# Routing the last two tiles from rows without norm, by folded router weights

## The chip, the cores and the metric

The kernel runs on one core of one Trainium2 chip. The metric is the device time of one execution in microseconds. Three runs of the kernel before gave 1399.96 us as median (1399.85 to 1399.97).

The engines are TensorE (PE; its weight loads are PEld), VectorE (DVE), ScalarE (ACT), GpSimd (POOL) and SyncE (SP), which here only issues transfers. Each has a queue of its own that it works off in order, and waits on semaphores for the others.

## The reference, cut to what matters

One decoder layer over 1024 tokens of 1024 columns. The change touches the end of the first half and the router of the mixture of experts:

```python
x = layer_norm(DN_ALPHA * x + merged @ w_out[l], ln1_g[l], ln1_b[l])
# hierarchical_moe(x): the best of 4 groups, then the best 2 of its 8 experts
glog = (xt @ w_rg + b_rg)                  # 4 columns
gval, gsel = lax.top_k(glog, 1)
elog = (xt @ w_re + b_re)                  # 32 columns
top_v, top_i = lax.top_k(elog_of_the_group, 2)
weights = softmax(glog)[gsel] * softmax(top_v)
y[token] = sum over its 2 experts of weight * (silu(x @ w_gate) * (x @ w_up)) @ w_down
x = layer_norm(DN_ALPHA * x + y, ln2_g[l], ln2_b[l])
```

The norm is `(u - mean) * rstd * g + b`. The 36 router logits of a token can therefore also be had from its row `u` without norm: with `W' = g * W`, from which the mean of its columns over the 1024 rows is taken, they are `rstd * (u @ W') + (b @ W + bias)`.

## The kernel before, in words

The stages are: projections and attention, the linear recurrence, mixing (up to some 740 us of the profiled execution), the experts (from 767), and the second norm at the end. All products in 32 bits are made of three TensorE passes over a high and a low part (lines 103 to 105); ScalarE makes the high part (L98), VectorE the low one (L99).

**Mixing** (`mixing`) works on 1024 tokens in two halves. A half has 8 branch products and then, for each of its 4 tiles of 128 tokens, two products with `w_out`, one for each 512 columns (`project`). Every product is cut in two parts of 12 passes or more, and such a part is a *tick*; ticks 0 to 63 hold all 32 products. Everything else is put in by tick: `before` holds loads, `stages` what follows a first part, `late_stages` what follows the tick's `post`. The engines' queues are in exactly this written order (`all_order`). After a tile's second product VectorE adds alpha times x and takes statistics (L840, L841, L918), GpSimd makes 1/sqrt (L701), and one or more ticks later `norm` scales the row (four operations, L925 and L926), and `store` writes it to HBM twice, as `x1d`, from which the experts' rows are gathered, and as `zd`, to which their results are added.

**Routing** (`router`) works on batches of two tiles, in five steps whose ticks stand in `BATCHES`: `turn` transposes the normed row (TensorE) and copies it out of PSUM (ScalarE); `logits` multiplies it by the 36 router columns; `choose` turns the logits back and finds group and experts by some 27 small VectorE operations; `place` ranks each token among those of its expert; `enter` adds a matmul to the table of places, which lies in PSUM. From the table `slots` takes the 32 lists of token numbers (`gi`, L1060) and starts the first two gathers of rows (L1086). All of `pa`, one bank of PSUM, is shared by logits, choices and ranks.

**Weights of the experts** are read in 384 pieces of 0.5 MB by SP's queue (`fetch`), into 36 buffers that they share with the tiles of mixing. Ten pieces are fetched in ticks 48 to 60, eight behind tile 6's store and ten behind tile 7's, 28 in all, before the experts begin. SP's queue also holds the stores of the normed rows. Behind the router stands a branch for experts of more than 128 tokens (`overflow`, L1377), which isn't taken; every engine reads one value for it, and at its end SP waits for all transfers that it has issued. Then a piece is fetched for each that is used. At the end of the queue, behind the last piece, stand the loads of `z` for the second norm (`final`).

`warm(n)` issues n small matmuls without use, after the ticks in `WARM`.

The code lines of the profile (L...) are those of this listing.

Of the kernel before, what the change touches and what calls it, by code (L numbers as in the profile page):

```python
# [5 lines left out]
F32 = mybir.dt.float32  # L6
F32R = mybir.dt.float32r
I32 = mybir.dt.int32
AF = mybir.ActivationFunctionType
ALU = mybir.AluOpType  # L10
AX = mybir.AxisListType
# [4 lines left out]
D = 1024  # L16
NE = 32
ALPHA = 2.0 ** 0.25
LN_EPS = 1e-5
# [42 lines left out]
class Builder:  # L62
# [48 lines left out]
    def warm(self, n):  # L111

        if n:
            ps = self.bank("mm")
            for _ in range(n):
                self.nc.tensor.matmul(ps[:, 0:128], self.c("ident"), self.c("ident"), start=True, stop=True)

    WARM = {63: 11, 65: 5, 66: 14, 67: 5}

    def pe_order(self):  # L120
        return self.tc.manual_schedule(engines={mybir.EngineType.PE})
# [641 lines left out]
    def mixing(self):  # L763


        nc = self.nc
        g1, b1 = self.x4(name="ln1_g"), self.x4(name="ln1_b")
        self.wr = self.tile([128, 8, 36], F32, "wr", 1)
        self.br = self.tile([36, 1], F32, "br", 1)

        def constants():
            for t, name in ((g1, "ln1_g"), (b1, "ln1_b")):
                nc.sync.dma_start(t, self.a[name].partition_broadcast(128))
            nc.sync.dma_start(self.wr, self.a["w_r"].rearrange("(k p) c -> p k c", p=128))
            nc.sync.dma_start(self.br, self.a["b_r"][:, None])

        self.asum = None
        self.table = self.bank("tb", (128, 64))
# [9 lines left out]
        def at(d, b, fn):  # L788
            d.setdefault(b, []).append(fn)
# [35 lines left out]
        def project(b, i, c):  # L825
            ps = self.bank("mm")
            s = slice((i % 4) * 128, (i % 4) * 128 + 128)
            for k in range(8):
                h, l = mg[k // 2]
                wh, wl = wo[4 * c + k // 2]  # L830
                self.mm3(ps, h[:, k % 2, s], l[:, k % 2, s], wh[:, k % 2], wl[:, k % 2], k == 0, k == 7)
                if k == 3:
                    yield
            if c == 0:
                u[i] = self.x4(name="u"), self.tile([128, 2, 6], F32, "lst", 2)

            def post():
                t, st = u[i]
                cs = slice(c * 512, c * 512 + 512)
                nc.vector.scalar_tensor_tensor(t[:, cs], xr[i][:, cs], ALPHA, ps, op0=ALU.mult, op1=ALU.add)  # L840
                nc.vector.bn_stats(st[:, c], t[:, cs])  # L841
                if c == 1:
                    mv = self.stats(st, LN_EPS)
                    self.at(2 * b + 2, lambda: norm(2 * b + 2, i, t, mv), True)

            return post

        def norm(b, i, t, mv):
            for c in range(2):
                self.scale(t, mv, g1, b1, c)  # L850
            self.at(b + 2 * (i < 7), lambda: store(i, t))
            batch = next(g for g in self.BATCHES if i in g[0])
            if i == batch[0][0]:
                self.batch = self.router(batch[0])
            for n, d in enumerate(batch[1]):
                fn = self.batch[n]
                if n < 2:
                    self.at(b + d, lambda fn=fn: fn(i, t))
                elif i == batch[0][-1]:
                    self.late_stages.setdefault(b + d, []).append(fn)  # L860

        def store(i, t):
            for d in (self.x1d, self.zd):
                nc.sync.dma_start(d[i * 128:i * 128 + 128, :], t)

        main = []
# [20 lines left out]
                at(before, b, lambda b: self.fetch())  # L887

        at(before, 6, lambda b: constants())
        tick, gen = 0, None  # L890
        while tick < 2 * len(main) or stages or self.late_stages:
            post = None
            if tick < 2 * len(main):
                if tick % 2 == 0:
                    for fn in before.pop(tick // 2, []):
                        fn(tick // 2)
                    gen = main[tick // 2](tick // 2)
                    next(gen)
                else:
                    post = self.run(gen)  # L900
            due = stages.get(tick, [])
            while due:
                due.pop(0)()
            stages.pop(tick, None)
            if post:
                post()
            for fn in self.late_stages.pop(tick, []):
                fn()
            self.warm(self.WARM.get(tick, 0))
            tick += 1  # L910
            if tick >= 2 * len(main) - 1:
                for _ in range(4 if tick < 2 * len(main) + 1 else 2):
                    self.fetch(True)

    def stats(self, st, eps):

# [17 lines left out]
    def small(self, n, nm, bufs=1):  # L934
        return self.tile([128] + (list(n) if isinstance(n, tuple) else [n]), F32, "r" + nm, bufs)

    BATCHES = ((0, 1), (4, 5, 6, 10, 14)), ((2, 3), (4, 5, 6, 10, 14)), ((4, 5), (2, 3, 4, 6, 7)), ((6, 7), (1, 2, 2, 3, 4))

    def router(self, batch):


        nc, vec, t = self.nc, self.nc.vector, self.small
        V = {}
# [1 line left out]
        n = len(batch)  # L945
        lT = self.tile([36, n, 128], F32, "rlT", 1)

        def turn(i, x1):
            V["xT", i] = []
            for j in range(2):  # L950
                ps = self.bank("pb", (128, 4, 128))
                for k in range(4):
                    nc.tensor.transpose(ps[:, k], x1[:, (4 * j + k) * 128:(4 * j + k + 1) * 128], self.c("ident"))
                xT = self.tile([128, 4, 128], F32, "rxT", 2)
                nc.scalar.copy(xT, ps)
                V["xT", i].append(xT)

        def logits(i, _):
            lg = self.pa[0:36, 0:128]
            for j, xT in enumerate(V.pop(("xT", i))):  # L960
                for k in range(4):
                    nc.tensor.matmul(lg, self.wr[:, 4 * j + k], xT[:, k], start=j + k == 0, stop=j == 1 and k == 3)
            nc.scalar.activation(lT[:, i - batch[0]], lg, AF.Identity, bias=self.br)

        def first_max(vals, w, nm, ix):

            mx = t((n, 1), nm + "m")
            vec.tensor_reduce(mx, vals, axis=AX.X, op=ALU.max)
            c = t((n, w), nm + "c")
            for k in range(n):  # L970
                vec.scalar_tensor_tensor(c[:, k], vals[:, k], mx[:, k], low[:, 0:w], op0=ALU.is_ge, op1=ALU.mult)
            vec.tensor_reduce(ix, c, axis=AX.X, op=ALU.min)
            return mx

        def choose():
            l = self.pa[:, 128:128 + 36 * n].rearrange("p (n c) -> p n c", n=n)
            for k in range(n):
                nc.tensor.transpose(l[:, k], lT[:, k], self.c("ident")[0:36, 0:36])
            gl, el = l[:, :, 0:4], l[:, :, 4:36]
            gi = t((n, 1), "gi")  # L980
            gm = first_max(gl, 4, "g", gi)
            em, ge, gs, d = t((n, 32), "em"), t((n, 4), "ge"), t((n, 1), "gs"), t((n, 1), "dd")
            for k in range(n):
                vec.tensor_scalar(em[:, k], self.c("group"), gi[:, k], -3.0e38, op0=ALU.not_equal, op1=ALU.mult)
            vec.tensor_sub(ge, gl, gm.to_broadcast([128, n, 4]))
            nc.scalar.activation(ge, ge, AF.Exp)
            vec.tensor_add(em, em, el)
            eid = self.eid[:, batch[0]:batch[0] + n]
            oh = t((n, 2, 32), "oh")
            ms = []  # L990
            for j in range(2):
                ms.append(first_max(em, 32, "ab"[j], eid[:, :, j:j + 1]))
                for k in range(n):
                    vec.tensor_scalar(oh[:, k, j], low, eid[:, k, j:j + 1], None, op0=ALU.is_equal)
                for k in range(n if j == 0 else 0):
                    vec.scalar_tensor_tensor(em[:, k], oh[:, k, 0], -3.0e38, em[:, k], op0=ALU.mult, op1=ALU.add)
            asg = t((n, 32), "asg")
            vec.tensor_add(asg, oh[:, :, 0], oh[:, :, 1])
            vec.tensor_sub(d, ms[1], ms[0])
            nc.scalar.activation(d, d, AF.Exp)  # L1000
            sums = [self.asum]
            for k in range(n):
                new = t(32, "sum", 6)
                if sums[-1] is None:
                    vec.tensor_copy(new, asg[:, k])
                else:
                    vec.tensor_add(new, sums[-1], asg[:, k])
                sums.append(new)
            self.asum = sums[-1]
            vec.tensor_reduce(gs, ge, axis=AX.X, op=ALU.add)  # L1010
            V["r"] = asg, oh, sums, gs, d

        def place():
            asg, oh, sums, gs, d = V["r"]
# [468 lines left out]
def arrays(inputs):  # L1483
# [10 lines left out]
        "w_out": f["w_out"][0],  # L1494
        "ln1_g": f["ln1_g"][0],
        "ln1_b": f["ln1_b"][0],
        "w_r": np.concatenate([f["router_group_w"][0], f["router_expert_w"][0]], axis=1),
        "b_r": np.concatenate([f["router_group_b"][0], f["router_expert_b"][0]]),
        "w_g": gate_up(f["w_exp_gate"][0]),
# [20 lines left out]
```

## Time and profile before

| | |
|---|---|
| median of three runs | 1399.96 us |
| profiled execution | 1399.95 us |
| its span | 1398.2 us |
| TensorE busy | 1335.6 us (96%) |
| VectorE busy | 1080.5 us (77%) |
| ScalarE busy | 789.4 us (56%) |
| bytes of all transfers | 327.84 MB, 234 GB/s on the mean |

All times are from the span's start; 1.75 us of the profiled execution lie around the span. An engine that is busy nearly all the time isn't thereby the bound: matmuls are pipelined and their ends modelled, and stages differ. In the rows further down, a window's DMA share is the mean busy share of the core's 16 DMA engines; a timeline row has start, length, engine, line, operation, out<-in with shapes, how many are merged (x2), and in brackets the idle time of the engine before it with what ended it; a row of waits has who waited <- for whom: total us, times, longest.

### The profile page before, as it was taken

To read this page: it belongs to the slowest core of one execution; us is meant where nothing else is said; L and a number is where in the kernel's file an instruction comes from. 1 tells how busy PE (TensorE), PEld (TensorE's weight loads), DVE (VectorE), ACT (ScalarE), POOL (GpSimd) and SP (SyncE) were. 2 spreads that over 40 slices of the span, in tenths; PEclk is the share of its full clock that TensorE was granted. 3 is DMA by queue.
4 is the path that set the end of the run, shared out by engine and by line. 5 is a ranking of instruction groups with operands and counts; after the bars stand their busy time and mean duration, and the time that the engine had idled before them with its cause. 6 is when DMAs were issued, how large, how long until landed. Compare 5 with 4: busy or idle time off the path is not lost. (4 is left out here: it accounts for less than half of the span.)

```text
span 1398.2 us, 22818 instructions
## 1 busy us (share of the span) xinstructions
PE 1335.6 (96%) x8314; PEld 1100.5 (79%) x8314; DVE 1080.5 (77%) x1798; ACT 789.4 (56%) x1282; POOL 241.8 (17%) x160
## 2 busy tenths in 40 slices
PE   7999999999999999999998999999999999999844
PEld 5888899987788887788787888888888888888621
DVE  4268985779989956668656989999999999999645
ACT  4367644335545532312112888888888888888542
POOL 0001312120000002300001122222222222222123
PEclk9999999999999999999999999999999999999967
DMA  6124232153444436763557999999999999999962
GB/s 246 56 89 145 100 112 76 39 169 114 137 128 146 148 103 194 254 211 121 196 195 287 356 368 369 366 356 354 353 357 358 352 358 357 367 360 365 369 251 97
DMA packets 142564, 327.84 MB, mean 234 GB/s; under 512 B 18614, under 2 KB 59702, under 8 KB 142448
## 3 DMA queue, kind: packets, MB, share of 16 engines
q1 hardware_dynamic: 132800, 308.78, 60.9%
q0 software_dynamic: 9648, 17.57, 4.9%
q8 instruction: 66, 1.08, 0.3%
q14 instruction: 50, 0.41, 0.1%
HBM read 291.43 MB, written 52.43 MB: 246 GB/s over the span
## 5 line engine op out<-in xcount | busy, mean ns | idle before, releaser
L99 DVE TENSOR_TENSOR el<-er,eh 128x1024 fp32r<-128x1024 f32 x368 | 436.8, 1223 | 53.4 <-ACT eh L98 37.8
L98 ACT CAST eh<-er 128x1024 fp32r<-128x1024 f32 x368 | 369.7, 1054 | 99.5 <-PE mm L104 82.7
L103 PE MATMUL mm<-xh,wh 128*128 128x512 f32 x480 | 194.9, 406 | 7.8 <-ACT wh L98 6.8
L103 PE MATMUL mm<-eh,xh 128*128 128x512 f32 x496 | 196.4, 396 | 0.0
L104 PE MATMUL mm<-el,xh 128*128 128x512 f32 x496 | 196.2, 395 | 0.0
L105 PE MATMUL mm<-eh,xl 128*128 128x512 f32 x496 | 196.1, 395 | 0.0
L104 PE MATMUL mm<-xl,wh 128*128 128x512 f32 x480 | 189.0, 394 | 0.8 <-DVE xl L99 0.8
L105 PE MATMUL mm<-xh,wl 128*128 128x512 f32 x480 | 189.1, 394 | 0.0
L103 PEld LDWEIGHTS mm<-xh,wh 128*128 128x128 f32 x480 | 91.4, 190 | 25.7 <-ACT wh L98 6.8
L105 PEld LDWEIGHTS mm<-eh,xl 128*128 128x128 f32 x496 | 93.2, 188 | 22.5
L104 PEld LDWEIGHTS mm<-el,xh 128*128 128x128 f32 x496 | 93.2, 188 | 22.3
L103 PEld LDWEIGHTS mm<-eh,xh 128*128 128x128 f32 x496 | 93.2, 188 | 22.3
L105 PEld LDWEIGHTS mm<-xh,wl 128*128 128x128 f32 x480 | 91.2, 190 | 20.6 <-DVE wl L99 0.8
L1086 POOL DMA_INDIRECT xg<-x1d,gi x32 | 58.1, 1816 | 279.3 <-PE pb L1149 255.4
L104 PEld LDWEIGHTS mm<-xl,wh 128*128 128x128 f32 x480 | 91.4, 190 | 17.7 <-DVE xl L99 1.1
L103 PE MATMUL mm<-eh,hth 128*128 128x512 f32 x240 | 100.2, 418 | 0.0
L1090 POOL DMA_INDIRECT zd<-y,gi x29 | 69.8, 2407 | 156.5 <-ACT y L1240 156.5
L105 PE MATMUL mm<-eh,htl 128*128 128x512 f32 x240 | 94.8, 395 | 0.0
L104 PE MATMUL mm<-el,hth 128*128 128x512 f32 x240 | 94.8, 395 | 0.0
L103 PE MATMUL mm<-wh,xh 128*128 128x256 f32 x256 | 73.1, 286 | 0.0
L105 PE MATMUL mm<-wh,xl 128*128 128x256 f32 x256 | 72.4, 283 | 0.0
L104 PE MATMUL mm<-wl,xh 128*128 128x256 f32 x256 | 72.4, 283 | 0.0
(257 smaller groups left out, 2522.7 us busy)
## 6 DMA issues: line engine op xcount, KB each, us to landing
er<-w_g SPq DMA_DIRECT2D x128, 512.0 KB
er<-w_u SPq DMA_DIRECT2D x128, 512.0 KB
er<-w_d SPq DMA_DIRECT2D x128, 512.0 KB
wr<-w_in SPq DMA_DIRECT2D x38, 512.0 KB
gated<-st SPq DMA_DIRECT2D x32, 256.0 KB
st<-gated SPq DMA_DIRECT2D x32, 256.0 KB
xr<-xt SPq DMA_DIRECT2D x8, 512.0 KB
wab<-w_a SPq DMA_DIRECT2D x16, 256.0 KB
```

The lines of the kernel that those rows point to most:

```text
L98: self.nc.scalar.copy(hi, src)
L99: (eng or self.nc.vector).tensor_sub(lo, src, hi.bitcast(F32))
L103: mm(out, lh, rh, start=start, stop=False)
L104: mm(out, lh, rl, start=False, stop=False)
L105: mm(out, ll, rh, start=False, stop=stop)
L1086: self.nc.gpsimd.indirect_dma_start(to, None, rows, bass.IndirectOffsetOnAxis(ap=self.column(self.gi, e), axis=0), bounds_check=T - 1, oob ...
L1090: self.nc.gpsimd.indirect_dma_start(self.zd, bass.IndirectOffsetOnAxis(ap=idx, axis=0), y, None, bounds_check=T - 1, oob_is_err=False, com ...
```

## The change

Tiles 6 and 7 are routed from the row without norm. `fold` and `centre` (ticks 16 to 20) make the folded weights `gwr` and the constant `shift` from the router weights and the norm's g and b, which come as a second, small input `ln1_gb`. In `raw`, which takes the place of `norm` for these two tiles, each 512-column half is transposed as soon as it is summed; the logits are made by `gwr`; `choose` now works on some of the batch's tiles, here on one, and multiplies by rstd and adds `shift` itself. Tile 6's choice comes before tile 7's. Tile 7's norm is cut in two: the first half runs before its choice, the second between choice and placing. The batch of tiles 4 and 5 moves one tick ahead. Of the pieces of weights, four (was eight) are fetched between the stores of tiles 6 and 7 and fifteen (was ten) behind the latter. The warming matmuls are no longer set by tick.

```diff
-    WARM = {63: 11, 65: 5, 66: 14, 67: 5}
...
+            nc.sync.dma_start(gb, self.a["ln1_gb"])
+            self.shift = self.tile([128, 36], F32, "wshift", 1)
+            nc.sync.dma_start(self.shift, self.a["b_r"].partition_broadcast(128))
+
+        def fold():
+            vec = nc.vector
+            self.gwr = self.tile([128, 8, 36], F32, "gwr", 1)
+            work = self.tile([128, 512], F32, "hh", 2)
+            bwr = work[:, 0:288].rearrange("p (k c) -> p k c", k=8)
+            sums = work[:, 288:360].rearrange("p (j c) -> p j c", j=2)
+            for j, w in enumerate((self.gwr, bwr)):
+                vec.tensor_mul(w, self.wr, gb[:, j, :, None].to_broadcast([128, 8, 36]))
+                vec.tensor_reduce(sums[:, j], w.rearrange("p k c -> p c k"), axis=AX.X, op=ALU.add)
+            return work
+
+        def centre(work):
+            vec, ps = nc.vector, self.pa[:, 0:72]
+            nc.tensor.matmul(ps, self.c("ones"), work[:, 288:360], start=True, stop=True)
+            for k in range(8):
+                vec.scalar_tensor_tensor(self.gwr[:, k], ps[:, 0:36], -1.0 / D, self.gwr[:, k], op0=ALU.mult, op1=ALU.add)
+            vec.tensor_add(self.shift, ps[:, 36:72], self.shift)
...
                 nc.vector.bn_stats(st[:, c], t[:, cs])
-                if c == 1:
+                if i >= 6:
+                    raw(2 * b + 2, i, t, st, c)
+                elif c == 1:
                     mv = self.stats(st, LN_EPS)
                     self.at(2 * b + 2, lambda: norm(2 * b + 2, i, t, mv), True)
...
+        def raw(b, i, t, st, c):
+            if i == 6 and c == 0:
+                self.batch = self.router((6, 7))
+            turn, logits, choose, place, enter = self.batch
+            if c == 0:
+                self.at(b, lambda: turn(i, t, (0,)), True)
+                if i == 7:
+                    self.at(b + 1, lambda: logits(i, (0,), self.gwr))
+                return
+            if i == 6:
+                self.at(b, lambda: turn(i, t, (1,)), True)
+                mv = self.stats(st, LN_EPS)
+                self.at(b + 1, lambda: logits(i, (0, 1), self.gwr), True)
+                self.at(b + 1, lambda: [self.scale(t, mv, g1, b1, c) for c in range(2)])
+                self.at(b + 2, lambda: choose(0, 1, mv))
+                self.at(b + 3, lambda: store(i, t), True)
+                return
+            turn(i, t, (1,))
+            mv = self.stats(st, LN_EPS)
+            self.warm(3)
+            logits(i, (1,), self.gwr)
+            self.scale(t, mv, g1, b1, 0)
+            choose(1, 2, mv)
+            self.scale(t, mv, g1, b1, 1)
+            self.warm(14)
+            place()
+            store(i, t)
+            self.warm(7)
+            enter()
...
+        self.at(16, lambda: self.at(20, lambda work=fold(): centre(work)))
...
             stages.pop(tick, None)
+            if tick == 2 * len(main) - 1:
+                for _ in range(4):
+                    self.fetch(True)
             if post:
                 post()
             for fn in self.late_stages.pop(tick, []):
                 fn()
-            self.warm(self.WARM.get(tick, 0))
             tick += 1
-            if tick >= 2 * len(main) - 1:
-                for _ in range(4 if tick < 2 * len(main) + 1 else 2):
-                    self.fetch(True)
+        for _ in range(self.NRAW):
+            self.fetch(True)
...
-    BATCHES = ((0, 1), (4, 5, 6, 10, 14)), ((2, 3), (4, 5, 6, 10, 14)), ((4, 5), (2, 3, 4, 6, 7)), ((6, 7), (1, 2, 2, 3, 4))
+    BATCHES = ((0, 1), (4, 5, 6, 10, 14)), ((2, 3), (4, 5, 6, 10, 14)), ((4, 5), (1, 2, 3, 5, 6))
...
-        def choose():
+        def choose(k0=0, k1=n, mv=None):
+            if k0 == 0:
+                V["r"] = t((n, 32), "asg"), t((n, 2, 32), "oh"), [self.asum], t((n, 1), "gs"), t((n, 1), "dd")
+            m, ks = k1 - k0, slice(k0, k1)
             l = self.pa[:, 128:128 + 36 * n].rearrange("p (n c) -> p n c", n=n)
-            for k in range(n):
+            for k in range(k0, k1):
                 nc.tensor.transpose(l[:, k], lT[:, k], self.c("ident")[0:36, 0:36])
+            l = l[:, ks]
+            if mv is not None:
+                l2 = t((1, 36), "l2")
+                vec.scalar_tensor_tensor(l2[:, 0], l[:, 0], mv[:, 1:2], self.shift, op0=ALU.mult, op1=ALU.add)
+                l = l2
+            asg, oh, sums, gs, d = V["r"]
+            asg, oh, gs, d = asg[:, ks], oh[:, ks], gs[:, ks], d[:, ks]
...
```

The rest of the diff hands halves of tiles (`js`), the weights (`w`) and the number of tiles (`m`) through `turn`, `logits`, `first_max` and `choose`; their operations stay.

SP's queue at the end of mixing, before, from tile 6's store to the branch; `u` is a tile's normed row, `er` a piece of expert weights, `cmi` the value that the branch reads:

```order
L864 DMA x1d<-u 128x1024
L864 DMA zd<-u 128x1024
L1127 DMA er<-w_g 128x1024 x2
L1127 DMA er<-w_u 128x1024 x4
L1124 DMA er<-w_d 128x1024 x2
L864 DMA x1d<-u 128x1024
L864 DMA zd<-u 128x1024
L1124 DMA er<-w_d 128x1024 x2
L1127 DMA er<-w_g 128x1024 x4
L1127 DMA er<-w_u 128x1024 x4
L1376 TENSOR_LOAD cmi
```

And after:

```order
L921 DMA x1d<-u 128x1024
L921 DMA zd<-u 128x1024
L1196 DMA er<-w_g 128x1024 x2
L1196 DMA er<-w_u 128x1024 x2
L921 DMA x1d<-u 128x1024
L921 DMA zd<-u 128x1024
L1196 DMA er<-w_u 128x1024 x2
L1193 DMA er<-w_d 128x1024 x4
L1196 DMA er<-w_g 128x1024 x4
L1196 DMA er<-w_u 128x1024 x4
L1193 DMA er<-w_d 128x1024
L1445 TENSOR_LOAD cmi
```

Four pieces stand between the two stores, where eight stood, and fifteen behind the second, where ten stood.

VectorE's queue after, from the last operations of the choice of tiles 4 and 5 to the placing of these tiles; `rgs` and `rsum` end a choice, `u<-u,...` is tile 6's norm, `u<-xr,mm` the sum of tile 7's first half, `rpay` begins the placing:

```order
L1077 TENSOR_TENSOR rsum<-rsum,rasg 128x32 x2
L1080 TENSOR_REDUCE rgs<-rge 128x2
L984 SCALAR_TENSOR_TENSOR u<-u,lmv,ln_g 128x512
L985 SCALAR_TENSOR_TENSOR u<-u,lmv,ln_b 128x512
L984 SCALAR_TENSOR_TENSOR u<-u,lmv,ln_g 128x512
L985 SCALAR_TENSOR_TENSOR u<-u,lmv,ln_b 128x512
L862 SCALAR_TENSOR_TENSOR u<-xr,mm 128x512
L863 BN_STATS lst<-u 128x6
L1093 TENSOR_SCALAR rpay<-roh,const 128x2x32 x2
```

The same place before, where the choice of tiles 4 and 5 stands behind tile 6's norm:

```order
L925 SCALAR_TENSOR_TENSOR u<-u,lmv,ln_g 128x512
L926 SCALAR_TENSOR_TENSOR u<-u,lmv,ln_b 128x512
L968 TENSOR_REDUCE rgm<-pa 128x2
L971 SCALAR_TENSOR_TENSOR rgc<-pa,rgm,const 128x4 x2
L972 TENSOR_REDUCE rgi<-rgc 128x2
L984 TENSOR_SCALAR rem<-const,rgi 128x32 x2
```

Tile 6's norm has moved from ahead of that choice to behind it.

VectorE's queue after, at the end of tile 7; the first rows are its last sum and statistics, `rl` its logits:

```order
L862 SCALAR_TENSOR_TENSOR u<-xr,mm 128x512
L863 BN_STATS lst<-u 128x6
L977 BN_AGGR lmv<-lst 128x2
L698 TENSOR_SCALAR lmv<-lmv 128x1
L984 SCALAR_TENSOR_TENSOR u<-u,lmv,ln_g 128x512
L985 SCALAR_TENSOR_TENSOR u<-u,lmv,ln_b 128x512
L1048 SCALAR_TENSOR_TENSOR rl_7919<-pa,lmv,wshift 128x36
L1030 TENSOR_REDUCE rgm<-rl_7919 128x1
```

Only half of the norm's four operations now stand ahead of the choice; the other two follow its last operation, ahead of the second placing.

## Rows read from the trace of the kernel before

**Rows 1.** Windows: stretch, its us, busy (instructions) by engine, PEclk, DMA share, GB/s

```profile
728.00:743.00 15.00, 14.49 (x93) 12.46 (x92) 10.89 (x49) 1.74 (x5) 0.65 (x1) 1.00 0.93 351
743.00:747.00 4.00, 2.66 (x23) 2.29 (x22) 2.17 (x3) 1.17 (x2) 2.05 (x3) 1.00 0.17 67
747.00:764.00 17.00, 14.02 (x118) 13.01 (x116) 11.49 (x51) 3.94 (x7) 3.19 (x2) 1.00 0.96 366
764.00:769.00 5.00, 4.09 (x28) 3.78 (x29) 2.66 (x4) 4.38 (x6) 0.99 (x1) 1.00 0.32 75
769.00:800.00 31.00, 31.00 (x147) 25.33 (x146) 28.61 (x29) 26.34 (x31) 2.82 (x2) 1.00 0.97 357
800.00:900.00 100.00, 100.00 (x463) 81.37 (x462) 89.45 (x87) 80.90 (x99) 23.41 (x11) 1.00 1.01 367
900.00:1330.00 430.00, 423.01 (x1967) 344.45 (x1965) 378.71 (x370) 341.42 (x415) 100.20 (x47) 1.00 0.99 359
```

**Rows 2.** Waits of SP's queue in 770:900, the longest

```profile
SPq L1127 <- PE mm L105: 61.2, 47, 2.8
```

**Rows 3.** Waits of SP's queue in 900:1330, the longest two

```profile
SPq L1124 <- DMA er<-w_g: 103.3, 83, 3.4
SPq L1127 <- DMA er<-w_u: 96.5, 85, 3.3
```

**Rows 4.** Waits of TensorE and of ScalarE in 770:1398

```profile
PE mm L1187 <- ACT xh L1158: 23.0, 1, 23.0
...
ACT w L1318 <- DMA z<-zd: 25.6, 1, 25.6
```

**Rows 5.** Timeline of SP's queue

```profile
727.54 0.32 SPq L864 DMA_DIRECT2D x1d<-u  x1
...
745.53 0.33 SPq L864 DMA_DIRECT2D x1d<-u  x1
...
767.63 3.85 SPq L1124 DMA_DIRECT2D er<-w_d  x4
...
1332.61 9.19 SPq L1309 DMA_DIRECT2D z<-zd  x8
```

**Rows 6.** Timeline of VectorE

```profile
722.36 0.69 DVE L840 SCALAR_TENSOR_TENSOR u<-xr,mm 128x512 f32<-128x512 f32 x1 [4.92 <-PE mm L105]
...
724.13 0.74 DVE L925 SCALAR_TENSOR_TENSOR u<-u,lmv,ln_g 128x512 f32<-128x512 f32 x1
...
740.37 0.69 DVE L840 SCALAR_TENSOR_TENSOR u<-xr,mm 128x512 f32<-128x512 f32 x1 [0.71 <-PE mm L105]
...
744.75 0.75 DVE L926 SCALAR_TENSOR_TENSOR u<-u,lmv,ln_b 128x512 f32<-128x512 f32 x1
750.13 0.17 DVE L968 TENSOR_REDUCE rgm<-pa 128x2 f32<-128x8 f32 x1 [4.63 <-PE pa L978]
...
751.85 0.41 DVE L971 SCALAR_TENSOR_TENSOR rac<-rem,ram,const 128x32 f32<-128x32 f32 x2
...
755.25 0.41 DVE L1024 TENSOR_SCALAR rpay<-roh,const 128x64 f32<-128x64 f32 x2
...
758.88 0.19 DVE L1060 TENSOR_SCALAR gi<-tb 128x32 int32<-128x32 f32 x1 [0.61 <-PE tb L1047]
```

**Rows 7.** Timeline of TensorE (a transpose of four blocks, logits, the experts' start)

```profile
745.65 0.63 PE L953 MATMUL pb<-const,u 128*128 128x128 f32 x4 [0.82 <-DVE u L926]
...
747.32 1.94 PE L962 MATMUL pa<-rxT,wr 128*36 128x128 f32 x16
...
764.91 1.07 PE L1149 MATMUL pb<-const,xg 128*128 128x128 f32 x8 [1.33 <-DMA xg<-x1d,gi]
...
767.07 0.47 PE L103 MATMUL mm<-eh,xh 128*128 128x512 f32 x1
```

**Rows 8.** Timeline of GpSimd: the first gather of the experts' rows

```profile
759.95 1.46 POOL L1086 DMA_INDIRECT xg<-x1d,gi  x1 [14.90 <-DVE tw L1061]
```

**Rows 9.** All gathers into xg, from issue to landing

```profile
DMA to landing us min/median/max: 4.7/8.3/9.0
```

More of the change, by code (lines that the diff above doesn't have):

```diff
@@ L769, in mixing @@
         self.br = self.tile([36, 1], F32, "br", 1)
+        gb = self.tile([128, 2, 8], F32, "gb", 1)
         def constants():
@@ L850, in norm @@
                 self.scale(t, mv, g1, b1, c)
-            self.at(b + 2 * (i < 7), lambda: store(i, t))
+            self.at(b + 2, lambda: store(i, t))
             batch = next(g for g in self.BATCHES if i in g[0])
@@ L856, in norm @@
                 fn = self.batch[n]
-                if n < 2:
+                if n == 0:
                     self.at(b + d, lambda fn=fn: fn(i, t))
+                elif n == 1:
+                    self.at(b + d, lambda fn=fn: fn(i))
                 elif i == batch[0][-1]:
@@ L946, in router, with turn @@
         lT = self.tile([36, n, 128], F32, "rlT", 1)
-        def turn(i, x1):
-            V["xT", i] = []
-            for j in range(2):
+        def turn(i, x1, js=(0, 1)):
+            for j in js:
                 ps = self.bank("pb", (128, 4, 128))
@@ L953, in turn, with logits, first_max @@
                     nc.tensor.transpose(ps[:, k], x1[:, (4 * j + k) * 128:(4 * j + k + 1) * 128], self.c("ident"))
[L954 to L958, printed above, removed]
+                V["xT", i, j] = self.tile([128, 4, 128], F32, "rxT", 2)
+                nc.scalar.copy(V["xT", i, j], ps)
+        def logits(i, js=(0, 1), w=None):
             lg = self.pa[0:36, 0:128]
-            for j, xT in enumerate(V.pop(("xT", i))):
+            for j in js:
+                xT = V.pop(("xT", i, j))
                 for k in range(4):
[L962 to L967, printed above, removed]
+                    nc.tensor.matmul(lg, (self.wr if w is None else w)[:, 4 * j + k], xT[:, k], start=j + k == 0, stop=j == 1 and k == 3)
+            if js[-1] == 1:
+                if w is None:
+                    nc.scalar.activation(lT[:, i - batch[0]], lg, AF.Identity, bias=self.br)
+                else:
+                    nc.scalar.copy(lT[:, i - batch[0]], lg)
+        def first_max(vals, m, w, nm, ix):
+            mx = t((n, 1), nm + "m")[:, 0:m]
             vec.tensor_reduce(mx, vals, axis=AX.X, op=ALU.max)
-            c = t((n, w), nm + "c")
-            for k in range(n):
+            c = t((n, w), nm + "c")[:, 0:m]
+            for k in range(m):
                 vec.scalar_tensor_tensor(c[:, k], vals[:, k], mx[:, k], low[:, 0:w], op0=ALU.is_ge, op1=ALU.mult)
@@ L973, in first_max @@
             return mx
-        def choose():
+        def choose(k0=0, k1=n, mv=None):
+            if k0 == 0:
+                V["r"] = t((n, 32), "asg"), t((n, 2, 32), "oh"), [self.asum], t((n, 1), "gs"), t((n, 1), "dd")
+            m, ks = k1 - k0, slice(k0, k1)
             l = self.pa[:, 128:128 + 36 * n].rearrange("p (n c) -> p n c", n=n)
-            for k in range(n):
+            for k in range(k0, k1):
                 nc.tensor.transpose(l[:, k], lT[:, k], self.c("ident")[0:36, 0:36])
+            l = l[:, ks]
[5 more added lines that the diff above has]
+            asg, oh, gs, d = asg[:, ks], oh[:, ks], gs[:, ks], d[:, ks]
@@ L979, in choose @@
             gl, el = l[:, :, 0:4], l[:, :, 4:36]
[L980 to L983, printed above, removed]
+            gi = t((n, 1), "gi")[:, 0:m]
+            gm = first_max(gl, m, 4, "g", gi)
+            em, ge = t((n, 32), "em")[:, 0:m], t((n, 4), "ge")[:, 0:m]
+            for k in range(m):
                 vec.tensor_scalar(em[:, k], self.c("group"), gi[:, k], -3.0e38, op0=ALU.not_equal, op1=ALU.mult)
-            vec.tensor_sub(ge, gl, gm.to_broadcast([128, n, 4]))
+            vec.tensor_sub(ge, gl, gm.to_broadcast([128, m, 4]))
@@ L986, in choose @@
             nc.scalar.activation(ge, ge, AF.Exp)
             vec.tensor_add(em, em, el)
-            eid = self.eid[:, batch[0]:batch[0] + n]
-            oh = t((n, 2, 32), "oh")
+            eid = self.eid[:, batch[k0]:batch[k0] + m]
             ms = []
             for j in range(2):
-                ms.append(first_max(em, 32, "ab"[j], eid[:, :, j:j + 1]))
-                for k in range(n):
+                ms.append(first_max(em, m, 32, "ab"[j], eid[:, :, j:j + 1]))
+                for k in range(m):
@@ L994, in choose @@
                     vec.tensor_scalar(oh[:, k, j], low, eid[:, k, j:j + 1], None, op0=ALU.is_equal)
-                for k in range(n if j == 0 else 0):
+                for k in range(m if j == 0 else 0):
                     vec.scalar_tensor_tensor(em[:, k], oh[:, k, 0], -3.0e38, em[:, k], op0=ALU.mult, op1=ALU.add)
-            asg = t((n, 32), "asg")
             vec.tensor_add(asg, oh[:, :, 0], oh[:, :, 1])
@@ L1000, in choose @@
             nc.scalar.activation(d, d, AF.Exp)
-            sums = [self.asum]
-            for k in range(n):
+            for k in range(m):
                 new = t(32, "sum", 6)
@@ L1010, in choose @@
             vec.tensor_reduce(gs, ge, axis=AX.X, op=ALU.add)
-            V["r"] = asg, oh, sums, gs, d
         def place():
@@ L1496, in arrays @@
         "ln1_b": f["ln1_b"][0],
+        "ln1_gb": np.ascontiguousarray(np.stack([f[k][0].reshape(8, 128).T for k in ("ln1_g", "ln1_b")], axis=1)),
         "w_r": np.concatenate([f["router_group_w"][0], f["router_expert_w"][0]], axis=1),
```

## The prediction, written before the changed kernel was timed

> **What bounds the kernel now.** I read the windows by stage first, then the waits of SP's queue, then the waits at the end, then the row-by-row timelines of 722 to 768 us.
>
> The change sits between the mixing stage and the experts. VectorE takes up tile 7's last product at 740.37 [rows 6], and TensorE starts the first expert product at 767.07 [rows 7]. These 26.7 us look like the thing to shorten. The windows say that something else runs through the expert stage at its limit: the DMA share is 0.97, 1.01 and 0.99 in 769:800, 800:900 and 900:1330 [rows 1]. SP's queue tells who holds whom. In 770:900 its weight loads wait for TensorE to free a buffer (61.2 us) [rows 2]; from 900 on they wait for earlier weight loads to land (103.3 and 96.5 us, and a third such row) [rows 3]. So the DMA engines fall behind while they are full, and from 900 they set the pace.
>
> The end of the kernel hangs on that stream. The eight loads of z stand behind the last weight load in SP's queue and go out at 1332.61 [rows 5]; ScalarE waits 25.6 us for the first, and TensorE stands 23.0 us behind ScalarE [rows 4]. TensorE thus has 23 us in hand at the end, the DMA stream none. What counts is how long the DMA engines stand empty before the experts, not when TensorE starts on them.
>
> From 728 to 800 that emptiness, (1 - share) x length, is 1.05 + 3.3 + 0.7 + 3.4 + 0.9 = 9.4 us [rows 1]. The 3.3 lie before the store of tile 7, the 3.4 where SP stops at the overflow branch and loads again at 767.63 [rows 5].
>
> **The change, part by part.** SP's queue is in order: a store that waits for its tile holds all weight loads behind it. Before, tile 6's store goes out at 727.54, eight weight loads follow, tile 7's store goes out at 745.53, and ten follow [rows 5]. After, four loads stand between the two stores and fifteen behind the second, as the order shows. So I need the two times at which the norms end on VectorE.
>
> Tile 6. TensorE now does the logits of tile 5 (1.94 us) and four transposes (0.63) [rows 7] before the half product that VectorE's operation at 722.36 waits for [rows 6]: 724.9. To the end of its statistics, 1.8 us (722.36 to 724.13 [rows 6]): 726.7. VectorE's order then has the choice of tiles 4 and 5 ahead of tile 6's norm: 5.1 us (750.13 to 755.25 [rows 6]): 731.8. The norm, four operations of 0.75 [rows 6]: 734.8. Tile 6's store goes out then, 7.3 us later than before.
>
> Tile 7. VectorE goes on: sum and statistics of its first half 1.4 us (2 x 0.69 [rows 6]): 736.2; placing tiles 4 and 5, 3.0 (755.25 to 758.88, less 0.6 for entering the table): 739.2; the new choice of tile 6 alone. No row has a choice of one tile. Bounds: the 5.1 of two tiles, and half of it, 2.6. Of 27 operations 8 second ones of a pair fall away (a pair takes 0.41 [rows 6], the second overlapping the first: I take 0.16 each) and one is added (0.25): 4.1, nearest the upper end. That is 743.3. TensorE's last product is later too: added before it are logits and transposes, 4 more transposes and the entries of tiles 4 and 5, some 2 us, so it ends near 742.5 and hides behind VectorE. Tile 7's last sum starts at 743.4, against 740.37 [rows 6]: 3.0 us lost before the chain begins.
>
> The chain: sum 0.7, hand-over 0.15: transposes at 744.25. From the second transposes to the choice was 4.5 us (745.65 [rows 7] to 750.13 [rows 6]); half the logits (1.0) and some 0.3 of waiting fall away: 747.5. Choice 4.1: 751.6. The norm's second half, which now stands between choice and placing, 2 x 0.75: 753.1. Here tile 7's store goes out, 7.6 us later than before. Placing and entering 3.6: 756.7; to the gather 1.1 (758.88 [rows 6] to 759.95 [rows 8]): 757.8. The gather leaves 2.2 us earlier, and that is all that the shorter chain leaves.
>
> DMA engines. Traffic starts about 0.8 us after a store's issue (743:747 has 0.7 us of it, after 745.53 [rows 1, 5]). Empty from 728 to 735.6: 7.6 us. Two stores and four loads of 0.524 MB at 366 GB/s [rows 1] take 8.6: to 744.2. Empty to 753.9: 9.7. Two stores and fifteen loads: 24.3 us, to 778, the gathers between them. At the overflow branch SP drains its queue and refills: before, 3.4 us; after, it reaches the branch late, with loads outstanding, so what is left is issue and first packet. Bounds 0 and 4; I take 2. Sum 19.3, less 9.4: the stream is 9.9 us later, and as its share is full from there on, so is the end.
>
> The Trainium skill (DMA: Bandwidth & Descriptors, "Where 436 GB/s comes from") says that HBM binds a core's loads at about 358 GB/s. The trace agrees for 900:1330 (359) and lies above it in 747:764 and 800:900 (366, 367) [rows 1]. By the page the six transfers take 8.8 us and the empty time after them is 9.5, so the sum would be 9.7.
>
> The folding (13 operations of 36 to 288 columns, between 0.15 and 0.75 us each, one small matmul, two small loads) lies in ticks 16 to 20 beside the branch products of TensorE; 0 if hidden, 4 us on every later time if not. I take 0.
>
> The profiled execution took 1399.95 us around a span of 1398.2, the runs' median is 1399.96; so 1399.95 + 9.9 = 1409.9 us. Its own range: the choice of one tile at its lower bound, twice, takes 3 from the second store and 1.5 from the first; refilling gives -2 to +2; unhidden folding +4: 1404 to 1416.
>
> **Rivals.** *TensorE's start sets the end.* Up to 900 SP waits for TensorE [rows 2]; if the 28 loads fetched ahead cover what the stream loses, the end moves with the first expert product. The gather leaves 2.2 us earlier. Landing now takes 5.0 (759.95 [rows 8] to 764.91 [rows 7]); if it stays so: 1397.8. Among fifteen loads it may be nearer the usual 8.3 [rows 9], +3.3: 1401.1. It decides as long as the loads stay ahead of TensorE to the end. Against it: the 23 us in hand [rows 4].
>
> *The same, with VectorE not behind.* If tile 7's sum still starts at 740.4, the gather leaves 5.2 earlier: 1394.8. This wants the bound on the choice halved and TensorE's added work absorbed; the forecast's own DMA term, still several us, speaks against it.
>
> *The drain costs more.* If SP, stopped at the branch until all fifteen have landed near 778, then needs its whole 4 us again, and the gathers in that stretch slow the loads by 2: +14, 1414.
>
> **How the numbers follow.** Forecast 0.71; drain 0.09; TensorE's start 0.12, half of it with the gather unslowed; VectorE not behind 0.08. About 0.2% (2.8 us) is what a measurement of this kernel can tell from no change. Slower: 0.71 + 0.09 = 0.80. TensorE's start gives 0.08 of same, the rest goes with the 0.08 as faster: 0.12. The range: 1401, the upper end of TensorE's start, to 1416. The forecast alone: 1404 to 1416.
>
> **What would show it.** Right: tile 6's store near 735, tile 7's near 753, no DMA traffic between about 744 and 754; SP waiting for landings and not for TensorE already in 800:900; the z loads near 1342; TensorE's wait at the end still above 20 us though its first expert product comes no later than 768. Wrong: stores at the times of before, or z loads at 1333 with a late store (the loads catch up), or TensorE's end wait shrunk by what it starts later.

## The result, and the profile after

The changed kernel took 1409.76 us (median of four runs, 1408.10 to 1411.18) against 1399.97 before: a ratio of 1.0068, 95% interval 1.005 to 1.0085. It is slower, and 0.1 us from the forecast; but two terms of the forecast were too small, not all of the empty time reached the end, and one of its readings was wrong. The profiled execution took 1409.93 us around a span of 1408.2.

Windows of the kernel after, to be held against [rows 1] (same columns):

```profile
728.00:735.60 7.60, 7.20 (x44) 5.68 (x43) 7.01 (x32) 1.14 (x4) 0.55 (x1) 1.00 0.00 0
735.60:744.00 8.40, 8.01 (x44) 6.39 (x44) 7.74 (x37) 0.79 (x2) 0.00 (x0) 1.00 0.85 301
744.00:754.00 10.00, 9.04 (x75) 8.17 (x74) 8.85 (x35) 3.16 (x7) 2.70 (x3) 1.00 0.16 64
754.00:764.00 10.00, 7.79 (x53) 7.41 (x52) 6.48 (x23) 2.40 (x3) 3.19 (x2) 0.83 0.96 345
764.00:769.00 5.00, 2.67 (x22) 2.65 (x23) 1.29 (x2) 2.00 (x4) 0.98 (x1) 1.00 1.03 392
769.00:800.00 31.00, 31.00 (x147) 25.30 (x147) 27.86 (x28) 25.47 (x30) 2.85 (x2) 1.00 0.83 323
800.00:900.00 100.00, 100.00 (x462) 81.39 (x461) 91.47 (x89) 83.58 (x100) 16.08 (x11) 1.00 1.00 371
900.00:1330.00 430.00, 423.76 (x1961) 342.83 (x1960) 384.74 (x372) 349.40 (x416) 69.42 (x46) 1.00 0.99 360
```

No transfer runs for 7.6 us, hardly one in 744:754, and 0.17 of 769:800 is empty again. SP's queue, whose rows answer to [rows 5], says why:

```profile
736.12 0.32 SPq L921 DMA_DIRECT2D x1d<-u  x1
...
739.06 0.92 SPq L1196 DMA_DIRECT2D er<-w_u  x2
753.76 0.33 SPq L921 DMA_DIRECT2D x1d<-u  x1
...
771.39 14.14 SPq L1193 DMA_DIRECT2D er<-w_d  x4
...
784.24 1.30 SPq L1193 DMA_DIRECT2D er<-w_d  x3
...
1342.31 9.22 SPq L1378 DMA_DIRECT2D z<-zd  x8
```

The stores of tiles 6 and 7 go out 8.6 and 8.2 us later than before. The row at 771.39 merges the one load ahead of the branch with three behind it; a narrower view shows these three, from 784.24. The queue reaches the branch while its loads are still under way and is free again at 784.24 (767.63 before). The loads of z leave 9.7 us later, and so the kernel ends. VectorE, to be held against [rows 6]: tile 6's norm at 733.05 behind the choice of tiles 4 and 5, the choice of tile 6 alone from 740.28, tile 7's last sum right behind it, and the placing of tiles 6 and 7 from 753.64:

```profile
726.16 0.69 DVE L862 SCALAR_TENSOR_TENSOR u<-xr,mm 128x512 f32<-128x512 f32 x1 [7.48 <-PE mm L105]
...
733.05 0.74 DVE L984 SCALAR_TENSOR_TENSOR u<-u,lmv,ln_g 128x512 f32<-128x512 f32 x1
...
740.28 0.25 DVE L1048 SCALAR_TENSOR_TENSOR rl<-pa,lmv,wshift 128x36 f32<-128x36 f32 x1
...
744.35 0.68 DVE L862 SCALAR_TENSOR_TENSOR u<-xr,mm 128x512 f32<-128x512 f32 x1
...
753.64 0.41 DVE L1093 TENSOR_SCALAR rpay<-roh,const 128x64 f32<-128x64 f32 x2
```

Then GpSimd's first gather, which answers to [rows 8], and TensorE's transposes of it and first expert product, which answer to [rows 7]:

```profile
758.35 1.47 POOL L1155 DMA_INDIRECT xg<-x1d,gi  x1 [9.32 <-DVE tw L1130]
```

```profile
766.33 1.06 PE L1218 MATMUL pb<-const,xg 128*128 128x128 f32 x8 [2.72 <-DMA xg<-x1d,gi]
...
768.49 0.48 PE L103 MATMUL mm<-eh,xh 128*128 128x512 f32 x1
```

The gather leaves 1.6 us earlier than before, but what it reads is there 8.0 us later instead of 5.0, with fifteen loads beside it: TensorE starts 1.4 us later. SP's waits in 770:900 (those of [rows 2]) and the waits at the end (of [rows 4]):

```profile
SPq L1196 <- DMA er<-w_d: 28.2, 23, 3.5
SPq L1193 <- DMA er<-w_g: 28.0, 25, 2.8
SPq L1196 <- DMA er<-w_u: 27.3, 24, 2.0
SPq L1446 <- SPq L1446: 11.7, 7, 2.8
SPq L1196 <- PE mm L105: 2.7, 7, 0.7
```

```profile
PE mm L1256 <- ACT xh L1227: 23.3, 1, 23.3
```

```profile
ACT w L1387 <- DMA z<-zd: 27.0, 1, 27.0
```

SP now waits for landings from the first expert on; of its 61.2 us for TensorE 2.7 are left. L1446 is the branch: 11.7 us in seven waits for its own transfers.

### The profile page after: what moved, and what is told of

Its sections match the earlier page's. It is cut to its first block, busy times and chain, and to the rows that moved or that the text cites. A ratio compares the mean times of both kernels' runs of the same rounds, so it can differ in the third digit from the quotient of the medians.

```text
span 1408.2 us, 22844 instructions
## 1 busy us (share of the span) xinstructions
PE 1337.7 (95%) x8294; PEld 1097.5 (78%) x8294; DVE 1093.4 (78%) x1824; ACT 797.4 (57%) x1284; POOL 203.6 (14%) x160
## 5 line engine op out<-in xcount | busy, mean ns | idle before, releaser
L98 ACT CAST eh<-er 128x1024 fp32r<-128x1024 f32 x368 | 378.4, 1052 | 98.0 <-PE mm L104 48.9
L1159 POOL DMA_INDIRECT zd<-y,gi x29 | 54.9, 1893 | 218.0 <-ACT y L1309 218.0
L1155 POOL DMA_INDIRECT xg<-x1d,gi x32 | 36.6, 1143 | 261.7 <-PE pb L1218 243.8
```

Of the source, the lines that this page charges most:

```text
L98: self.nc.scalar.copy(hi, src)
L1155: self.nc.gpsimd.indirect_dma_start(to, None, rows, bass.IndirectOffsetOnAxis(ap=self.column(self.gi, e), axis=0), bounds_check=T - 1, oob ...
L1159: self.nc.gpsimd.indirect_dma_start(self.zd, bass.IndirectOffsetOnAxis(ap=idx, axis=0), y, None, bounds_check=T - 1, oob_is_err=False, com ...
```

## The experiments

The expectations weigh two theories. Theory A is the forecast's: the end follows the empty time of the DMA engines ahead of the experts. Theory B is the rival: the end follows TensorE's first expert product.

All ratios are to runs of the kernel before on the same chip; their medians were 1399.97 to 1401.02 us, so the ratios compare, and the medians only roughly. The last three columns are from timelines of the profiled executions: start of the first expert product, issue of the z loads, and what lies between.

| kernel | median us | ratio (95%) | start | z loads | between |
|---|---|---|---|---|---|
| before | 1399.97 | | 767.07 | 1332.61 | 565.5 |
| after | 1409.76 | 1.0068 (1.005, 1.0085) | 768.49 | 1342.31 | 573.8 |
| e1 before, pieces 4 and 15 | 1404.99 | 1.0035 (1.0021, 1.0048) | 773.18 | 1338.42 | 565.2 |
| e2 after, pieces 10 and 9 | 1401.29 | 1.001 (1.0001, 1.0019) | 768.84 | 1333.72 | 564.9 |
| e4 after, stores by ScalarE | 1397.29 | 0.9981 (0.997, 0.9993) | 765.81 | 1329.69 | 563.9 |
| e5 after, TensorE late | 1409.04 | 1.0064 (1.0049, 1.0079) | 775.53 | 1341.52 | 566.0 |
| e6 after, no branch | 1405.65 | 1.003 (1.002, 1.004) | 768.74 | 1338.45 | 569.7 |
| e7 after, tile 6's norm first | 1411.13 | 1.0069 (1.0055, 1.0083) | 771.97 | 1343.33 | 571.4 |
| e8 before, stores by ScalarE | 1400.30 | 0.9997 (0.9988, 1.0007) | 767.38 | 1332.87 | 565.5 |
| e9 before, TensorE late | 1406.06 | 1.0036 (1.0024, 1.0049) | 770.67 | 1336.98 | 566.3 |
| e10 as e4, warmed longer | 1397.62 | 0.9979 (0.997, 0.9988) | 766.04 | 1329.97 | 563.9 |
| e11 as e4, 30 pieces | 1402.46 | 1.0016 (1.0002, 1.0029) | 768.47 | 1334.31 | 565.8 |

**TensorE's start: e5 and e9.** The same edit in the kernel after and in the kernel before:

```diff
-        self.warm(6)
+        self.warm(26)
         post()
```

> The changed kernel with 20 more warming matmuls ahead of the first expert product, which then starts some 5 us later (about 773.5). Nothing on the DMA side ahead of it changes. Theory A: SP's queue is stopped until 784 anyway and the stream is behind TensorE after that, so 1410 (1408.5 to 1411.5), and TensorE's wait at the end shrinks by about 5 us from 23.3. Theory B: 1414 to 1415.

> The kernel before with the same 20 warming matmuls ahead of the first expert product that left the changed kernel where it was. Here all 28 pieces have landed by then and SP's queue waits for TensorE to free buffers (61.2 us in 770:900), so theory A with full buffers says that each us of TensorE's start is a us of empty DMA engines: the start moves by 5 to 8 us, the end with it: 1406 (1404.5 to 1408.5). If only stores and the branch could hold the stream: 1400 to 1401.

In the kernel after, TensorE started 7.0 us later and the time stayed: its start does not set the end there. (Its gather was used 9.6 us after its issue, which adds to the 20 warming matmuls.) The rest of the expectation failed: TensorE's wait at the end didn't shrink (23.4). The 7 us went where TensorE had waited for pieces; its busy time in 900:1330 rose from 423.76 to all of it:

```profile
900.00:1330.00 430.00, 430.00 (x1995) 349.81 (x1995) 391.54 (x377) 354.68 (x423) 69.93 (x48) 1.00 0.99 358
```

In the kernel before, the start moved by 3.6 us, less than expected, the z loads by 4.4 and the time by 0.36% (5.0 us). There SP waits for TensorE throughout 770:900:

```profile
SPq L1127 <- PE mm L105: 58.7, 48, 2.8
SPq L1124 <- PE mm L105: 29.6, 27, 3.9
```

So the stream has two holders. Where the loads are ahead, SP waits for TensorE to free buffers (45 to 63 us on the longest such row in 770:900), and "between" is 564 to 566 in each of these eight kernels: before, e1, e2, e4, e8 to e11. There each us of TensorE's start is about a us of the end. In the kernel after it is 573.8 with 2.7 us of such waits: the late loads hold the stream, and TensorE has some 8 us to spare, of which e5 took 7 (566.0).

**The order of stores and loads: e1, e2, e4, e8.** e1 gives the kernel before the new split of the pieces; e2 fills the gap of the kernel after:

```diff
# e1, in the kernel before
-                for _ in range(4 if tick < 2 * len(main) + 1 else 2):
+                for _ in range(0 if tick == 2 * len(main) else 4):
                     self.fetch(True)
# e2, in the kernel after
-                for _ in range(4):
+                for _ in range(10):
                     self.fetch(True)
```

> The kernel before with one edit: four pieces (was eight) fetched between the stores of tiles 6 and 7, fifteen (was ten) behind the latter, as in the changed kernel; norms, router and TensorE's order are untouched. Theory A (the end follows the empty time of the DMA engines before the experts): four pieces of 1.43 us fewer ahead of the store of tile 7 leave 5.7 us more empty there; 17 transfers behind 745.5 end near 770 and SP's branch stops the queue near 771 to 773 instead of 767.6, with one piece more fetched (1.6 us): 1403 to 1406, SP waiting for landings already in 800:900. Theory B (TensorE's first expert product sets the end): its chain is untouched, so 1400, or at most 1403 where the gather is slowed by the loads.

> The changed kernel with ten pieces (was four) between the stores of tiles 6 and 7, nine (was fifteen) behind the latter. Theory A: the DMA engines work through 744 to 753.7, where they stood empty for 8.4 us; behind the store of tile 7 the transfers end near 770 and the queue starts again near 774 instead of 784. The end comes some 8 us earlier: 1401.5 (1400 to 1404). Theory B: TensorE's start moves by no more than the gather gains from fewer loads beside it (up to 3 us): 1407 to 1410.

e2 met its number: with 744:754 at a share of 0.87 and 769:800 at 0.91, 0.58% (8.1 us) of the loss is gone, though nothing in VectorE's or TensorE's order changed:

```profile
744.00:754.00 10.00, 7.56 (x62) 6.76 (x60) 8.82 (x40) 3.64 (x7) 2.70 (x3) 1.00 0.87 347
...
769.00:800.00 31.00, 31.00 (x146) 25.30 (x146) 26.55 (x27) 24.67 (x29) 2.81 (x2) 0.99 0.91 345
```

e1 met its number too, but can't tell the theories apart: TensorE's start moved by 6.1 us with it, since the gather's rows came late and the transposes took 1.94 us instead of 1.07:

```profile
769.03 1.94 PE L1149 MATMUL pb<-const,xg 128*128 128x128 f32 x8 [5.92 <-DMA xg<-x1d,gi]
```

"Between" is 565.2 there, and SP waits 46.2 us for TensorE in 770:900, though theory A had it waiting for landings from 800 on: this kernel's end follows TensorE.

```profile
SPq L1127 <- PE mm L105: 46.2, 27, 2.9
```

e4 and e8 take the two stores out of SP's queue:

```diff
-                nc.sync.dma_start(d[i * 128:i * 128 + 128, :], t)
+                (nc.scalar if i >= 6 else nc.sync).dma_start(d[i * 128:i * 128 + 128, :], t)
```

> The changed kernel with the stores of tiles 6 and 7 issued by ScalarE's queue, so that no load of SP's queue stands behind a store. Theory A: the loads go as their buffers come free, from about 727; all 28 or 29 have landed by about 758, SP's queue is stopped at the branch no later than before (767.6) and starts with one piece more: 1397.5 (1396 to 1401). The store of tile 7 may land later, beside loads, and its gather by some 2 us. Theory B: 1407 to 1411, as TensorE's start moves by at most the gather's 3 us.

> The kernel before with the stores of tiles 6 and 7 issued by ScalarE's queue. Its 28 pieces had landed ahead of the first expert product anyway, so the stream waits for TensorE's start, which this leaves at about 767: 1400 (1398.5 to 1401.5) on theory A with full buffers. If the folded routing is worth nothing once no load stands behind a store, this ties with the changed kernel with the same edit (1397.3); if its shorter chain counts there, this is 1.5 to 3 us above that.

Both met their numbers. The loads of e4 run on as buffers come free, and the DMA engines are full up to 754 (the row at 743.33 merges one load ahead of the branch with three behind it):

```profile
728.88 2.21 SPq L1193 DMA_DIRECT2D er<-w_d  x4
735.17 2.10 SPq L1196 DMA_DIRECT2D er<-w_g  x4
738.22 4.11 SPq L1196 DMA_DIRECT2D er<-w_u  x4
743.33 25.86 SPq L1193 DMA_DIRECT2D er<-w_d  x4
```

```profile
744.00:754.00 10.00, 7.60 (x62) 6.80 (x61) 8.82 (x40) 1.97 (x6) 2.70 (x3) 1.00 1.00 394
754.00:764.00 10.00, 7.54 (x61) 7.38 (x62) 4.91 (x11) 4.15 (x6) 3.15 (x3) 0.95 0.28 93
```

The share of 0.28 behind that shows no cost: the pieces due ahead of the branch have all gone out, and from 770 on SP waits mostly for TensorE, not for landings:

```profile
SPq L1196 <- PE mm L105: 45.4, 26, 2.9
```

e4 is 0.19% faster than the kernel before and 0.16% ahead of e8, whose interval holds 1. The intervals of e4 and e8 just overlap; that of e10 below, which has the same stores, ends where e8's begins. So the folded routing seems to gain some 0.2%, once no load stands behind a store. The whole loss of the kernel after comes from those two stores' place ahead of the loads in SP's queue.

**The stop at the branch: e6.** Edit: `overflow` returns at once.

> The changed kernel without the branch for experts of more than 128 tokens (the computation for them is left out; with these inputs the branch isn't taken), so that SP's queue never stops for its transfers. It sizes the forecast's term for the stop. Theory A with the size that the changed kernel's window shows (0.17 of 31 us in 769:800, 5.3 us empty): these go, the DMA share of 769:800 rises to 0.97 or more, 1405 (1403.5 to 1406.5). With the forecast's 2 us: 1408. Theory B: TensorE starts at the same time: 1409 to 1410.

769:800 is full, the z loads leave 3.9 us earlier, and the ratio falls by 0.0038, 5.3 us. That is nearer the size that the window shows (0.17 x 31 = 5.3) than the forecast's 2:

```profile
769.00:800.00 31.00, 31.00 (x145) 25.29 (x145) 26.39 (x27) 24.66 (x29) 2.82 (x2) 0.98 1.03 408
```

**Tile 6's store alone: e7.**

```diff
-                self.at(b + 1, lambda: [self.scale(t, mv, g1, b1, c) for c in range(2)])
+                self.scale(t, mv, g1, b1, 0), self.scale(t, mv, g1, b1, 1)
...
-                self.at(b + 3, lambda: store(i, t), True)
+                self.at(b, lambda: store(i, t), True)
```

> The changed kernel with tile 6's norm ahead of the choice of tiles 4 and 5 on VectorE, and its store a tick sooner; the store of tile 6 then goes out near 731.5 instead of 736.1, that of tile 7 as before (753.8). Theory A: the four pieces only move 4.6 us forward, the empty time ahead of them turns into empty time behind them, and the end stays: 1409.5 (1408 to 1411). If the late store of tile 6 by itself were what costs: 1405.

The norm here also stands ahead of the transposes of tile 6's second half, so its tokens get other logits and experts. The store left at 730.29, 5.8 us sooner, and nothing was gained: 744:754 fell to a share of 0.01. Tile 7's store left at 755.22, 1.5 us later than in the kernel after, and the median lies just above the expected range. With four pieces between the stores, an earlier first store only moves the gap. (TensorE's start, 3.5 us later here, was to spare.)

**Towards a better version: e10, e11.** e10 is e4 with `warm(30)` for `warm(20)` at the end of `slots`, e11 is e4 with `NRAW = 30`.

> The changed kernel with the stores of tiles 6 and 7 on ScalarE's queue, and ten more warming matmuls at the end of the router, which fill most of TensorE's 2.4 us of waiting for the first gather; after that wait its granted clock was 0.76 in 764:769, and transposes and warming took 1.5 us longer than in the kernel before. Buffers are full by then, so the end should follow TensorE's start: 1 to 1.5 us earlier than with the stores alone, 1396 (1394.5 to 1398). If the stream alone sets the end: 1397.3, as there.

> The changed kernel with the stores of tiles 6 and 7 on ScalarE's queue and 30 pieces (was 29) fetched ahead of the branch, which fills the 36 buffers. Where buffers are full the end should come one piece (1.57 us) earlier: 1395.7 (1394 to 1398). If the first three pieces' halves then wait for a buffer, TensorE starts later and it is 1397 to 1399.

e10 removed TensorE's idle time (granted clock 1.00 in 764:769, 0.76 in e4), but in the profiled execution its gather left 1.7 us later (758.57 against 756.84; tile 4's store was already 1.5 us later), so that its start is no earlier; its ratio can't be told from e4's. e4 and e10 beat both kernels. e11 was a miss: at the experts' start ScalarE stands waiting for TensorE to free a buffer for the next piece's high part, and TensorE is busy for 29.74 of 31 us in 769:800:

```profile
770.55 1.05 ACT L98 CAST eh<-er 128x1024 fp32r<-128x1024 f32 x1 [2.72 <-PE mm L104]
```

TensorE's own wait there is for VectorE (1.3 us), and that ScalarE's wait stands behind it is not shown. Its first gather also came late (TensorE waits 4.4 us for it). By the table, 2.7 of the 4.6 us by which its z loads leave later than e4's lie in TensorE's start, and 1.9 behind it.

## Why the prediction was right, and where it wasn't

*Right by its own steps.* The store of tile 6 came at 736.12 (forecast 734.8), of which 1.3 us is the sum at 726.16 (724.9); tile 7's last sum at 744.35 (743.4), its store at 753.76 (753.1), the gather at 758.35 (757.8). The choice of one tile takes 4.07 us to the next sum (740.28 to 744.35; forecast 4.1). The two gaps of the stores are 7.6 + 1.3 = 8.9 and 10 x 0.84 = 8.4 us, 17.3 together, the sum that the forecast had (7.6 + 9.7). e2, e4 and e7 show that it is these gaps, not the later norms themselves, that cost.

*Wrong in size: the stop at the branch.* Forecast 2 us between bounds of 0 and 4; window 5.3, e6 5.3 by its ratio (3.9 by its z loads). The queue reached the branch with loads outstanding, as foreseen, but that didn't shorten the restart: SP waits there for its transfers (11.7 us), the next load leaves at 784.24, and the window shows the DMA engines partly empty meanwhile.

*Wrong in size: the folding, taken as 0.* The store of tile 4, the last one ahead of the rearranged routing, leaves 1.2 us later than before (the first row is the kernel before, the second the kernel after):

```profile
701.86 0.33 SPq L864 DMA_DIRECT2D x1d<-u  x1
703.07 0.33 SPq L921 DMA_DIRECT2D x1d<-u  x1
```

From there to the sum at 726.16 pass 23.1 us, against 20.5 to the sum at 722.36 before: 2.6 more, as the forecast had it, so the 1.3 us by which that sum came late were there already. The delay arises where the folding is done. From the load of ln_g in SP's queue, ahead of it, to the store of tile 1, behind it, pass 32.9 to 33.0 us in the four kernels with the old routing, 34.4 in the kernel after, and 33.2 to 35.0 in the other seven that fold. So the stretch with the folding costs some 0.3 to 2.1 us more, by execution.

*What made up for it.* By the windows the empty time in 728:800 is 7.6 + 1.3 + 8.4 + 0.4 + 5.3 = 23.0 us (forecast 19.3), 13.6 more than before's 9.4; the end moved by 9.7. The forecast took each us of empty time for a us of the end. The same windows in bytes, before and after, come nearer:

```profile
728.00:800.00 72.00, 66.25 (x403) 56.87 (x402) 55.81 (x135) 37.57 (x49) 9.70 (x8) 1.00 0.87 322
728.00:800.00 72.00, 65.71 (x378) 55.61 (x377) 59.24 (x153) 34.98 (x47) 10.28 (x9) 0.98 0.69 258
```

At 800 the kernel after is (322 - 258) x 72 / 359 = 12.8 us behind. The windows behind that give back (371 - 367) x 100 / 359 = 1.1 and (360 - 359) x 430 / 359 = 1.2 us: 10.5 are left, as near to 9.7 as rates in whole GB/s can tell. Why the rates came out higher isn't shown; e2, e5, e6 and e7 have 358 in 900:1330, so this rate scatters between executions by as much. The closeness of the total was partly luck.

*Wrong as a reading: TensorE's 23 us in hand.* This wait is 20.9 to 23.9 us in all twelve kernels, whoever holds the stream, so it measures no slack. In the kernel before TensorE's start and the end move together (e9): the sentence that only the empty time counts, not TensorE's start, holds for the kernel after (e5) and not for the kernel before. The rival of TensorE's start thus lost here only because SP's queue came to be later than TensorE by some 8 us; in e1 SP's waits and "between" fit it.

*A signature missed.* The first expert product came at 768.49, not by 768: the gather among fifteen loads took 8.0 us, the +3.3 of that rival.

## What to carry to other kernels

A store in an in-order load queue is a barrier with the store's due time: when its work moves, count the loads on either side of it, or give it another queue. Empty time of a saturated stream costs only where the loads are what comes late; if the queue then waits for its consumer to free buffers, the consumer's start is the price. A long wait at the end is no slack until an experiment has delayed that engine.

## What the hardware showed that was not expected

The first gather's rows were in use 5.0 us after its issue in the kernel before and 8.0 in the kernel after. All twelve kernels divide in this way: 8.0 to 9.6 us in the six whose loads run on beside the gather (DMA share 0.87 to 1.03 in 764:769), 4.9 to 6.4 in the six others (0.32 to 0.61; in e9 and e10 TensorE itself came later than the rows). That the loads are the cause is argued from this alone. TensorE stands while it waits for these rows, and its clock can fall: after 4.4 us of waiting in e11 the granted clock of 764:769 was 0.50, the 1.2 GHz level, and the transposes behind it took 1.94 us instead of 1.07; in the kernel before, after 1.3 us of waiting, and in the kernel after, after 2.7, it was 1.00, in e4, after 2.4, 0.76. So a late gather can make the first product later still.

In 769:800 of e6 the DMA engines moved 408 GB/s; the Trainium skill (DMA: Bandwidth & Descriptors, "Where 436 GB/s comes from") gives about 358 as the bound of a core's loads, which the long window 900:1330 agrees with (360 in the kernel after) and such stretches do not.
